# Four moves in a two-layer FoX/YOCO trunk: GpSimd's computing in written order, half a panel behind a panel's reads, a hidden block's steps, and two products of a query pair

## The chip, the cores and the metric

One core of one Trainium2 chip runs the whole program. The metric is the device time of one execution in microseconds (us); the time of a kernel is the median of its runs.

## The reference

The input x is (1, 256, 2048) in float32; there are 16 heads of 128 and two layers.

```python
def sq_relu_mlp(h, g, w1, w2):
    a = jax.nn.relu(rms_norm(h, g) @ w1)
    return (a * a) @ w2
...
    for l in range(N_A):
        u = rms_norm(h, a_norm_g[l])
        proj = u @ a_w_in[l]
        q, k, v, fz = jnp.split(proj, [D, 2 * D, 3 * D], axis=-1)
        q = rms_norm(q.reshape(B, S, H, Dh), a_q_g[l])
        k = rms_norm(k.reshape(B, S, H, Dh), a_k_g[l])
        v = v.reshape(B, S, H, Dh)
        logf = jax.nn.log_sigmoid(fz.astype(jnp.float32) + a_b_f[l].astype(jnp.float32))
        o = forgetting_attention(q, k, v, logf)
        h = h + o.reshape(B, S, D) @ a_w_out[l]
        h = h + sq_relu_mlp(h, mlp_norm_g[layer], mlp_w1[layer], mlp_w2[layer])
        layer += 1
    kv = rms_norm(h, kv_norm_g) @ kv_w
    k_sh, v_sh = jnp.split(kv, [D], axis=-1)
    k_sh = rms_norm(k_sh.reshape(B, S, H, Dh), kv_k_g)
    v_sh = v_sh.reshape(B, S, H, Dh)
    for l in range(N_B):
        u = rms_norm(h, b_norm_g[l])
        q = rms_norm((u @ b_w_q[l]).reshape(B, S, H, Dh), b_q_g[l])
        o = chunked_relbias_attention(q, k_sh, v_sh, b_rel[l])
        h = h + o.reshape(B, S, D) @ b_w_out[l]
        h = h + sq_relu_mlp(h, mlp_norm_g[layer], mlp_w1[layer], mlp_w2[layer])
        layer += 1
    return h
```

The first layer attends causally with a bias made of summed log forget gates; the second attends in chunks of 64 with a learned bias by distance. N_A and N_B are 1, D is 2048, the hidden width of the MLP is 8192.

## The kernel before, in words

**Products.** All weights and activations are float32 and are split into a high and a low part: ACT writes the high part of a tile (`hi`, L323), DVE subtracts it from the tile and writes the low part (`lo`, L324). A product then takes three passes over TensorE, each a run of matmuls of 512 columns: high activation by high weight (L592), low activation by high weight (L594), high activation by low weight (L596). A run has four matmuls in an ordinary product and two in a product of a pair (below). The unit of weight is 128x1024, 512 KB; a unit's three passes of four matmuls each use one `hi` and one `lo`. Three `hi` and three `lo` buffers go round.

**Pairs.** Part of the weight columns are taken in pairs (`Pair`) by a scheme of the Strassen-Winograd kind. Four panels, 12, 22, 21 and 11, give seven products: 12, 11, 21, 22 and those of the sums T3 (22 and 12), T1 (12 and 11), T2 (T3 and 11) and T4X`bring` (L937) issues a panel's load on SP; `make` (L965) forms a sum on DVE; `put` (L975) forms one with an accumulating DMA that GpSimd issues, which reads the second panel from memory and adds it to the tile; T4 of an MLP's pair is made this way, each half when DVE has split T2's half. In an MLP the panels are twice as wide (128x2048, 1 MB) and are used in halves of 1024 columns. When "V" is in `p.has`, DVE (L1017) has formed the accumulator that the pair's later products add to; the code asserts this before ordinary products of the second column ("b early").

**Order of the work.** `plan` lists pairs and ordinary units in the order in which TensorE takes them; `run` walks that list and issues everything in program order. Ahead of a pair, `prepare(p, d)` counts down the ordinary units still to come (d) and brings or makes each panel at the count that a row of a table of numbers sets for it (`units`, in the order 12, 22, 21, 11, T3, T1; here `p.units[1]` is that of panel 22). `FO` sets the order of the last three products of a pair by kind of pair: "4" is panel 21's product, "5" is T4's and "6" is 22's; where a kind has no entry the order is 456. Kinds are named by `p.order`: "second" is the pair at each MLP's opening, "query" the pair of the second layer's query projection.

**Fill.** Everything that isn't a product (norms, attention, hidden blocks) is cut into small steps in the list `fill`; `run_fill` issues one entry after each product. So a step's entry says between which products its instructions stand on their engine.

- A head norm (`head_norm`, L660 to L674) squares on ACT, sums on DVE (L663), scales and adds on DVE (L667), raises to the power -1/2 on GpSimd (L668, tile `ss`), and scales rows on ACT (L674, `qn`). It does so for two blocks of rows.
- The bias of a head group in the first layer (`decay_bias`) is loaded by a DMA on GpSimd (L911, tile `nb`) and masked by two GpSimd instructions (L913, L916); DVE reads it at L738. In the second layer (`rel_bias`) tile `rb` is loaded (L1229), a corner is set by a GpSimd MEMSET (L1231), and DVE copies part of it (L1233).
- A turn (`carry`) writes a tile to memory (L450) and reads it back in four pieces in another order (L456), both on SP's queue. The activations of an MLP's input come so: y<-q (L417), act<-y (L420) on ACT, then act<-y on DVE (L421). A hop (`hop`, L466) does the same for a hidden block by 16 small copies within the core, on SP's and GpSimd's queues.
- A hidden block of an MLP (`take`): after its hop ACT applies relu (L1038), squares into the high part (L1043) and squares in place (L1045); DVE subtracts (L1049), and four sums (L395 to L398) with their split (L402, L405) prepare what the pairs' products with sums need. A row of a table gives the entries of hop, reads, relu, square, square, subtract and sums: `T0H` for the first block of the first MLP, `T0K` for that of the second.

**What pins the order.** At the end `keep_order(tc, engines)` (L88) adds a dependency from each instruction to the next one on its engine, for DVE, ACT, TensorE and SP, so that the scheduler keeps these four in written order. GpSimd isn't among them: there the scheduler may set a ready instruction ahead of one that was written earlier.

Of the kernel before, what the change touches and what calls it, by code (L numbers as in the profile page):

```python
# [27 lines left out]
UN = 1024  # L28
# [1 line left out]
TABLES = {  # L30
    "ATA": ((10, 13, 15, 19, 9), (9, 12, 15, 18, 12), (8, 13, 15, 19, 9), (9, 9, 12, 12, 9)),
    "ATB": ((11, 12, 14, 18, 9), (9, 13, 15, 17, 11), (9, 12, 15, 17, 10), (7, 10, 12, 12, 10)),
# [27 lines left out]
    "SHORT": ((4, 0, 0, 4, 7, 7, 7, 8, 11), (2, 2, 3, 3, 7, 7, 8, 11, 13), (4, 0, 0, 2, 6, 6), (0, 0, 1, 2, 4, 5)),  # L60
# [24 lines left out]
WIDE2 = (0, 1, 2, 3, 4, 5, 6, 7)  # L85


def keep_order(tc, engines):  # L88

    last = {}  # L90
    for i in tc.nc.cur_bb.bb.instructions:
        if i.engine in engines:
            if i.engine in last:
                tc.add_manual_dep(i, last[i.engine], mybir.DependencyInfo(mybir.DependencyClass.NoSync, mybir.DependencyReason.DATA),
                                  reason="written order")
            last[i.engine] = i.name
# [3 lines left out]
def trunk(ctx: ExitStack, tc: tile.TileContext, xT, xr, gs, hg, bf, wgate, w_in, w_oa, w1a, w1fa, w1sa, w2fa, w2sa,  # L100
          w_kv, w_qb, w_ob, w1b, w1fb, w1sb, w2fb, w2sb, rel, out):
    nc = tc.nc
    V, S, G, TE, SY = nc.vector, nc.scalar, nc.gpsimd, nc.tensor, nc.sync
# [305 lines left out]
    def room(tag, name, dtype=F32):  # L409
        return qkv.tile([P, DEEP], dtype, name=name, tag=tag, bufs=1)  # L410
# [63 lines left out]
    query = []  # L474
# [445 lines left out]
    def bring(p, name):  # L920
        if p.order == "out1":
            i = int(name in ("11", "21"))
            if i not in p.box:
                p.box[i] = acts.tile([P, DEEP], F32, name="wB", tag="act")
            p.t[name] = p.box[i][:, name[0] == "2" and UN or 0 :][:, :UN]
        elif p.order in LAZY:
            f, n = owner.get(p.rooms[name], (None, None))
            assert f is None or {"12": "T1", "21": "21", "11": "11", "22": "22"}[n] in f.issued, ("room busy", name, n)
            assert n != "11" or "T2" in f.has
            owner[p.rooms[name]] = p, name  # L930
            p.t[name] = sub(p.rooms[name])[:, UN:]
        elif p.order == "":
            p.t[name] = sub(p.rooms[name])[:, :UN]
        else:
            p.t[name] = room(p.rooms[name], "w" + name)
        p.has.add(name)
        SY.dma_start(p.t[name][:, : p.cols], p.big[name])  # L937

    def make(p, name, half=None):
        t = p.t  # L940
        if half == 1:
            pass
        elif name == "T3":
            if p.order in ("query", ""):
                t[name] = query_room(0)
            elif p.order == "kv0":
                t[name] = query_room(3)
            elif p.order in LAZY:
                t[name] = acts.tile([P, 2 * UN], F32, name="wT3", tag="act")[:, :UN]
            else:  # L950
                t[name] = prob.tile([P, 4 * UN], F32, name="wT3", tag="p", bufs=1) if p.order == "early" else room("bias", "wT3")
        else:
            t[name] = t[{"T1": "12", "T2": "T3", "T4": "11"}[name]]
        a, b = {"T1": ("12", "11"), "T3": ("22", "12"), "T2": ("T3", "11"), "T4": ("21", "T2")}[name]
        cols = slice(0, p.cols) if half is None else slice(half * UN, min(half * UN + UN, p.cols))
        d, a, b = (t[i][:, cols] for i in (name, a, b))
        if name == "T3":
            assert {"22", "12"} <= p.has and "T1" not in p.has, "T3 order"
        if name == "T1":
            assert "T30" in p.has and "T31" in p.has, ("T1 order", p.order, p.has, p.units, getattr(p, "at", 0))  # L960
        for k in (0, 1):
            if half in (None, k):
                p.has.add(name + str(k))
        p.has.add(name)
        V.tensor_tensor(d, a, b, op=ALU.add)  # L965
# [9 lines left out]
        G.dma_start(p.t[name][:, cols], p.big[other][:, cols], accum_op=ALU.add)  # L975

    def prepare(p, d):
        if p.deep and d == p.units[4] - 1:
            make(p, "T3", 1)
        for name, at in zip(("12", "22", "21", "11", "T3", "T1"), p.units):  # L980
            if d == at and p.deep and name == "T3":
                make(p, "T3", 0)
            elif d == at:
                (bring if name[0] != "T" else put if p.adds and name == "T1" else make)(p, name)

    def run(plan, open_pair, masks=None, follow=None):
        starts = [i for i, it in enumerate(plan) if it[1:] == (2, 0)] + ([len(plan)] if follow else [])
        for i, (p, q, u) in enumerate(plan):
# [24 lines left out]
            else:  # L1013
# [10 lines left out]
                for nxt in [j for j in starts if j > i][: 2 if follow else 1]:  # L1024
                    d = sum(1 for it in plan[i:nxt] if it[1] < 2)
                    prepare(plan[nxt][0] if nxt < len(plan) else follow, d)
# [69 lines left out]
    def sub(tag):  # L1096
        if tag not in halves_of:
            halves_of[tag] = room(tag, "R")
        return halves_of[tag]
# [33 lines left out]
    def heads(out):  # L1133
# [34 lines left out]
        def after():  # L1168
            prepare(plan_h[0][0], box[0])
            box[0] -= 1  # L1170
# [107 lines left out]
        return f  # L1278

    mlp(plan_b, x3, S3, st3, store)  # L1280
    keep_order(tc, (V.engine, S.engine, TE.engine, SY.engine))


def _cols_a(w, swap=False):
# [79 lines left out]
```

## Time and profile before

| | |
|---|---|
| Median of 3 runs | 2054.43 us (2053.61 to 2055.51) |
| The profiled execution's own time | 2056.59 us |
| Its span, first to last instruction | 2054.8 us |
| TensorE's granted clock | 1.000 |
| Busy: TensorE, DVE, ACT, GpSimd | 99%, 87%, 68%, 12% of the span |
| Moved by DMA | 557.78 MB, mean 271 GB/s |

An execution's time includes some 1.8 us around the span. In the rows of the timeline the columns are the start and the duration in us, the engine, the line of the kernel, the operation, the tile written and the tiles read, and the shape; x4 at the end counts neighbouring instructions of one form that are shown as one. In brackets stand the idle time of the engine before the row and what ended it, as far as the profile can tell. SPq is SP's DMA queue; PEld is the loading of weights into TensorE.

### The profile page before, as it was taken

The page shows a single profiled execution, that of the slowest core. Times are in us where ns is not written, and L with a number is a line of the kernel's source. Part 1 is how long each engine was busy: PE and PEld are TensorE (multiplying, and loading weights), DVE is VectorE, ACT ScalarE, POOL GpSimd, SP SyncE. Part 2 cuts the span into 40 slices and gives each one's busy share as a digit, 9 for nine tenths or more (in the row PEclk, how much of TensorE's full clock was granted, in tenths as well). Part 3 has the DMA queues.
Part 4 walks back from the last instruction along what each step waited for, and adds up shares of the span by engine and source line. Part 5 has one row for each costly group of instructions (what it writes and reads, how often), then busy time and mean ns, then how long its engine had stood idle before and what let it go on. Part 6 is the DMA issues. An engine that isn't in the chain of part 4 may idle for free.

```text
span 2054.8 us, 27097 instructions
## 1 busy us (share of the span) xinstructions
PE 2043.5 (99%) x9062; PEld 1689.0 (82%) x9062; DVE 1786.1 (87%) x2065; ACT 1404.5 (68%) x1805; POOL 248.3 (12%) x351
## 2 busy tenths in 40 slices
PE   9999999999999999999999999999999999999999
PEld 8888878878888888888878888888888888888887
DVE  7788888899898899899988787889988988988996
ACT  7766666677677676677778666667866676776764
POOL 1121010021111102101012111100111111111020
PEclk9999999999999999999999999999999999999999
DMA  8898898898888898898889989888998888888984
GB/s 321 261 296 275 264 275 248 295 272 262 300 258 281 259 300 275 242 294 272 264 245 300 275 251 282 260 267 282 289 292 266 270 262 292 261 285 262 296 260 148
DMA packets 175021, 557.78 MB, mean 271 GB/s; under 512 B 40592, under 2 KB 69152, under 8 KB 152096
## 3 DMA queue, kind: packets, MB, share of 16 engines
q1 hardware_dynamic: 153824, 464.99, 64.3%
q0 software_dynamic: 20768, 90.75, 22.7%
q8 instruction: 71, 1.16, 0.2%
q14 instruction: 70, 0.57, 0.1%
q10 hardware_dynamic: 288, 0.30, 0.0%
HBM read 516.07 MB, written 27.29 MB: 264 GB/s over the span
## 4 chain that ended last, share of the span: by engine, by line
PE 92%; DMA 3%; DVE 2%; issue 2%; ACT 1%; POOL 0%; SPq 0%; DVEq 0%; ACTq 0%; POOLq 0%
PE acc L596 21%; PE acc L592 21%; PE acc L594 21%; PE s L596 9%; PE s L592 9%; PE s L594 9%; DVE lo L324 1%; PE po L729 1%; PE po L766 1%; DMA w<-in_w1fb 0%; DMA q<-turn 0%; ACT hi L323 0%; DMA w<-in_w2fa 0%; DMA query<-in_w_qb 0%; PE po L728 0%
## 5 line engine op out<-in xcount | busy, mean ns | idle before, releaser
L324 DVE TENSOR_TENSOR lo<-raw,hi 128x1024 fp32r<-128x1024 f32 (+1 forms) x409 | 494.8, 1214 | 81.3 <-ACT hi L323 77.4
L323 ACT ACTIVATE hi<-raw 128x1024 fp32r<-128x1024 f32 (+1 forms) x409 | 429.6, 1054 | 188.7 <-PE acc L594 130.9
L592 PE MATMUL acc<-hi,act 128*128 128x512 f32 x1774 | 496.4, 393 | 2.1 <-ACT hi L323 1.0
L596 PE MATMUL acc<-lo,act 128*128 128x512 f32 x1774 | 491.1, 390 | 1.7 <-DVE lo L324 1.5
L594 PE MATMUL acc<-hi,act 128*128 128x512 f32 x1774 | 490.4, 389 | 0.1
L596 PEld LDWEIGHTS acc<-lo,act 128*128 128x128 f32 x1774 | 332.2, 188 | 73.6 <-DVE lo L324 4.6
L594 PEld LDWEIGHTS acc<-hi,act 128*128 128x128 f32 x1774 | 332.9, 188 | 70.1 <-DVE act L421 0.5
L592 PEld LDWEIGHTS acc<-hi,act 128*128 128x128 f32 x1774 | 331.5, 188 | 71.2 <-ACT hi L323 2.5
L323 ACT ACTIVATE hi<-w 128x1024 fp32r<-128x1024 f32 x254 | 267.0, 1058 | 123.2 <-PE acc L594 81.4
L324 DVE TENSOR_TENSOR lo<-wT,hi 128x1024 fp32r<-128x1024 f32 x220 | 267.1, 1222 | 66.5 <-ACT hi L323 61.7
L324 DVE TENSOR_TENSOR lo<-w,hi 128x1024 fp32r<-128x1024 f32 x254 | 305.8, 1219 | 14.7 <-ACT hi L323 12.5
L323 ACT ACTIVATE hi<-wT 128x1024 fp32r<-128x1024 f32 x220 | 232.2, 1060 | 101.9 <-PE acc L594 43.5
L592 PE MATMUL s<-hi,act 128*128 128x512 f32 x530 | 146.5, 392 | 2.2 <-ACT hi L323 2.2
L596 PE MATMUL s<-lo,act 128*128 128x512 f32 x530 | 145.1, 389 | 0.1
L594 PE MATMUL s<-hi,act 128*128 128x512 f32 x530 | 144.8, 388 | 0.0
L466 POOL DMA_DIRECT2D q<-z x192 | 95.5, 510 | 252.5 <-DVE z L440 216.4
L592 PEld LDWEIGHTS s<-hi,act 128*128 128x128 f32 x530 | 98.9, 188 | 23.2 <-ACT hi L323 3.1
L596 PEld LDWEIGHTS s<-lo,act 128*128 128x128 f32 x530 | 99.1, 188 | 21.3 <-DVE lo L324 1.0
L594 PEld LDWEIGHTS s<-hi,act 128*128 128x128 f32 x530 | 99.4, 188 | 20.6
L592 PE MATMUL s<-hi,S 128*128 128x512 f32 x288 | 89.6, 392 | 0.0
L594 PE MATMUL s<-hi,S 128*128 128x512 f32 x288 | 88.7, 389 | 0.0
L596 PE MATMUL s<-lo,S 128*128 128x512 f32 x288 | 88.7, 389 | 0.0
(217 smaller groups left out, 2291.4 us busy)
## 6 DMA issues: line engine op xcount, KB each, us to landing
raw<-in_w_in SPq DMA_DIRECT2D x75, 512.0 KB, 5.9
w<-in_w2fa SPq DMA_DIRECT2D x32, 1024.0 KB, 6.2
w<-in_w2fb SPq DMA_DIRECT2D x32, 1024.0 KB, 6.5
w<-in_w1fa SPq DMA_DIRECT2D x28, 1024.0 KB, 7.0
w<-in_w1fb SPq DMA_DIRECT2D x28, 1024.0 KB, 7.4
raw<-in_w2sa SPq DMA_DIRECT2D x52, 512.0 KB, 7.1
raw<-in_w2sb SPq DMA_DIRECT2D x50, 512.0 KB, 7.4
raw<-in_w_kv SPq DMA_DIRECT2D x48, 512.0 KB, 5.3
```

Of the source, the lines that this page charges most:

```text
L323: S.activation(hi[:, c], raw[:, c], AF.Copy)
L324: V.tensor_tensor(lo[:, c], raw[:, c], hi[:, c].bitcast(F32), op=ALU.subtract)
L466: (G if i % 2 else SY).dma_start(dst[32 * j : 32 * j + 32, i * n : (i + 1) * n], z[32 * i : 32 * i + 32, j * n : (j + 1) * n])
L592: TE.matmul(ps[:, cols], xh, cut(hi, j), start=first, stop=False, **kw)
L594: TE.matmul(ps[:, cols], xl, cut(hi, j), start=False, stop=False, **kw)
L596: TE.matmul(ps[:, cols], xh, cut(lo, j), start=False, stop=last, **kw)
L729: TE.matmul(s[:, P : 3 * P], q[:, a, P:T], k[:, a], start=True, stop=True)
L766: TE.matmul(po[:, :T], v[:, 0, a * P : (a + 1) * P], pT[:, :2], start=True, stop=False)
```

## The change

The change does four things.

1. `keep_order` also takes GpSimd, all but its DMAs: its computing instructions stay in written order among themselves.
2. In a pair of kind "second" (one in each MLP) the load of panel 11 is cut in two. The first 1024 columns are issued where the whole panel was, the second 1024 when panel 22 comes up, just ahead of it. In the first MLP the four reads of a turn lie between these places.
3. In the first row of `T0H`, relu goes from entry 6 to 5 and the sums' first step from entry 6 to 7; the entries of hop, squares, subtraction and the split of the sums stay.
4. `FO` gets an entry for "query": T4's product goes behind 22's, "465" in the place of the default.

```diff
-    "FO": {"second": "456", "ahead1": "456", "ahead0": "456", "deep1": "456", "deep0": "465"},
+    "FO": {"second": "456", "ahead1": "456", "ahead0": "456", "deep1": "456", "deep0": "465", "query": "465"},
...
-    "T0H": ((1, -1, 6, 6, 6, 6, 6, 8, 8), (0, -1, 4, 5, 6, 6, 7, 8, 8), (0, 4, 6, 7, 7, 7), (1, -1, 5, 5, 5, 5)),
+    "T0H": ((1, -1, 5, 6, 6, 6, 7, 8, 8), (0, -1, 4, 5, 6, 6, 7, 8, 8), (0, 4, 6, 7, 7, 7), (1, -1, 5, 5, 5, 5)),
...
-def keep_order(tc, engines):
+def keep_order(tc, engines, compute):
 
     last = {}
     for i in tc.nc.cur_bb.bb.instructions:
-        if i.engine in engines:
+        if i.engine in engines or i.engine == compute and "DMA" not in type(i).__name__:
...
         p.has.add(name)
-        SY.dma_start(p.t[name][:, : p.cols], p.big[name])
+        if p.order == "second" and name == "11":
+            p.has.add("11 half")
+            SY.dma_start(p.t[name][:, :UN], p.big[name][:, :UN])
+        else:
+            SY.dma_start(p.t[name][:, : p.cols], p.big[name])
...
     def prepare(p, d):
+        if d == p.units[1] and "11 half" in p.has:
+            p.has.remove("11 half")
+            SY.dma_start(p.t["11"][:, UN : p.cols], p.big["11"][:, UN : p.cols])
...
-    keep_order(tc, (V.engine, S.engine, TE.engine, SY.engine))
+    keep_order(tc, (V.engine, S.engine, TE.engine, SY.engine), G.engine)
```

The lines behind L934 move by 4, those behind the start of `prepare` by 7: `put` is L979 after the change, relu L1045.

On GpSimd, at the last head group of the first layer, before the change (cd is the bias in memory, `wT` and `R` are tiles of pairs):

```order
L975 DMA R<-in_w_oa 128x1024
L911 DMA nb<-cd 128x1536
L668 TENSOR_TENSOR ss<-ss,mhalf 128x4
L913 AFFINE_SELECT nb<-nb 128x4x128
L916 AFFINE_SELECT nb<-nb 128x4x128
L668 TENSOR_TENSOR ss<-ss,mhalf 128x4
L975 DMA wT_2419<-in_w_oa 128x1024
```

And after it, at the same place:

```order
L979 DMA R<-in_w_oa 128x1024
L911 DMA nb<-cd 128x1536
L668 TENSOR_TENSOR ss<-ss,mhalf 128x4 x2
L913 AFFINE_SELECT nb<-nb 128x4x128
L916 AFFINE_SELECT nb<-nb 128x4x128
L979 DMA wT_2419<-in_w_oa 128x1024
```

The second power goes ahead of the two masks. In head groups 1 and 2 the masks go behind both powers of the next norm likewise, and in the first group of the second layer the MEMSET of `rb` goes behind two more pairs of powers.

On SP, at the opening of the first MLP (w_3683 is panel 11, w_3717 panel 22), before:

```order
L450 DMA turn<-z 128x1024
L937 DMA w_3683<-in_w1fa 128x2048
L299 DMA raw<-in_w1a 128x1024
L456 DMA q<-turn 32x4x256 x4
L937 DMA w_3717<-in_w1fa 128x2048
L299 DMA raw<-in_w1a 128x1024
```

And after (panel 22 is w_3718 here):

```order
L450 DMA turn<-z 128x1024
L939 DMA w_3683<-in_w1fa 128x1024
L299 DMA raw<-in_w1a 128x1024
L456 DMA q<-turn 32x4x256 x4
L984 DMA w_3683<-in_w1fa 128x1024
L941 DMA w_3718<-in_w1fa 128x2048
L299 DMA raw<-in_w1a 128x1024
```

Half of panel 11 goes behind the four reads and a raw block. In the second MLP the second half goes behind the reads and two raw blocks in the same way.

On DVE, at the first hidden block of the first MLP (L1017 forms an accumulator; `w` and `wT` are a pair's panel and T4), before:

```order
L1049 TENSOR_TENSOR act<-q,act 128x1024
L395 TENSOR_TENSOR sum<-q 128x256
L396 TENSOR_TENSOR sum<-q,sum 128x256
L397 TENSOR_TENSOR sum<-q 128x256
L398 TENSOR_TENSOR sum<-q,sum 128x256
L324 TENSOR_TENSOR lo<-w_3754,hi 128x1024
L1017 TENSOR_TENSOR s<-s,p_3941 128x512
L324 TENSOR_TENSOR lo<-wT_3800,hi 128x1024 x2
```

And after:

```order
L1056 TENSOR_TENSOR act<-q,act 128x1024
L324 TENSOR_TENSOR lo<-w_3755,hi 128x1024
L1024 TENSOR_TENSOR s<-s,p_3942 128x512
L395 TENSOR_TENSOR sum<-q 128x256
L396 TENSOR_TENSOR sum<-q,sum 128x256
L397 TENSOR_TENSOR sum<-q 128x256
L398 TENSOR_TENSOR sum<-q,sum 128x256
L324 TENSOR_TENSOR lo<-wT_3801,hi 128x1024 x2
```

The four sums go behind the split of a panel's half and the accumulator. On ACT relu goes ahead of three instructions: a copy of an accumulator (L1030) and two `hi`. On TensorE, in the query pair, the two runs of T4's product and the two runs of 22's change places around one ordinary product between them.

## The prediction

> **What bounds the kernel now.** I read the page first, then the waits of TensorE, then the timeline around each of them, and the transfers of the stretch where the engines wait for one. The page's span and its row of engines:
>
> ```profile
> span 2054.8 us, 27097 instructions
> PE 2043.5 (99%) x9062; PEld 1689.0 (82%) x9062; DVE 1786.1 (87%) x2065; ACT 1404.5 (68%) x1805; POOL 248.3 (12%) x351
> ```
>
> TensorE is busy all but 11.3 us of 2054.8, and no edit removes a matmul. So the change can win only pauses of TensorE, and can lose only by making new ones. The waits of TensorE (us in total, times, the longest) name nearly all of the large ones:
>
> ```profile
> PE s L592 <- ACT hi L323: 2.2, 1, 2.2
> PE acc L596 <- DVE lo L324: 1.5, 2, 1.4
> PE acc L592 <- ACT hi L323: 1.0, 2, 0.6
> PE acc L592 <- ACT act L420: 0.9, 1, 0.9
> ```
>
> Each of the four edits sits at one of these rows. To price a pause I compare starts: when nothing waits, what follows a run of four 512-column matmuls starts 0.91 us after it (this row of the chain of waits), and what follows a run of two 0.45 us, half of it:
>
> ```profile
> 279.75 0.91 PE s L596 x4
> ```
>
> **Edit 1, GpSimd in written order.** The timeline at head group 3 (start, duration, engine, line; in brackets the idle time and its releaser):
>
> ```profile
> 268.27 1.03 POOL L668 TENSOR_TENSOR ss<-ss,mhalf 128x4 f32<-128x4 f32 x1 [2.87 <-DVE ss L667]
> 268.81 0.23 DVE L667 TENSOR_SCALAR ss<-ss,ex 128x4 f32<-128x4 f32 x1
> 271.85 0.64 POOL L913 TENSOR_SCALAR_AFFINE_SELECT nb<-nb 128x512 f32<-128x512 f32 x1 [2.55 <-DMA nb<-cd]
> 274.03 1.44 POOL L668 TENSOR_TENSOR ss<-ss,mhalf 128x4 f32<-128x4 f32 x1
> 275.51 1.14 ACT L674 ACTIVATE qn<-acc,ss 128x128 f32<-128x128 f32 x4 [3.90 <-POOL ss L668]
> 276.68 0.71 DVE L440 STREAM_TRANSPOSE z<-qn 128x512 f32<-128x512 f32 x1 [1.47 <-ACT qn L674]
> 277.62 1.23 DVE L324 TENSOR_TENSOR lo<-raw,hi 128x1024 fp32r<-128x1024 f32 x1 [0.23 <-ACT hi L323]
> 277.64 1.20 PE L592 MATMUL s<-hi,act 128*128 128x512 f32 x4 [2.21 <-ACT hi L323]
> ```
>
> The second power (ss) has its input at 269.04 (268.81 + 0.23), but stands behind two masks, and the first of these waits until 271.85 for its DMA. ACT is free at 271.61 (275.51 less 3.90) and idle until qn; the split hi<-raw is queued behind qn, and TensorE waits for it: 2.21 us, and a slow start, 1.20 us for the 0.91 of a run of four. That makes 2.5 us. Changed, the second power runs from 269.30 to 270.3 or 270.7 (1.03 or 1.44 long), before ACT is free. qn starts at 271.61 and all behind it on ACT 3.9 us sooner: hi<-raw ends near 273.7, and TensorE is due at 275.43 (277.64 less 2.21). Late next is DVE's half of that split: it ends at 278.85 now, and without the 1.47 us of idle time for qn and the 0.23 us for hi at 277.15; the third pass is due at 277.25 (275.43 and two passes of 0.91). It just fits. I take 2.5 us, and 2.2 as the lower end.
>
> The other places where GpSimd's order changes cost nothing as long as the work that now comes later has a far reader. In the shared K/V part the MEMSET of rb goes behind two pairs of powers (the tile's row has durations, first and last start; then the timeline):
>
> ```profile
> L1233 DVE COPY rb<-rb x4: 419/420/423, 1166.2 to 1307.4; 128x512 f32<-128x512 f32 x4
> 1147.90 2.69 POOL L668 TENSOR_TENSOR ss<-ss,mhalf 128x4 f32<-128x4 f32 x2 [0.88 <-DVE ss L667]
> ```
>
> It now comes after the pair that ends at 1150.6 (1147.90 + 2.69); its reader, DVE's COPY, first runs at 1166.2: 15 us of cover. If that is gone, DVE waits at the COPY, us for us.
>
> **Edit 2, half a block behind the reads.** The MLP's opening, first a row of the windows (the stretch, its length, busy time and count of TensorE, its weight loads, DVE, ACT, GpSimd, granted clock, DMA share, GB/s), then two of its transfers (count, size, median us from issue to landing):
>
> ```profile
> 388.00:400.00 12.00, 12.00 (x55) 9.94 (x54) 7.77 (x10) 5.11 (x6) 0.00 (x0) 1.00 1.02 300
> ```
>
> ```profile
> w<-in_w1fa SPq DMA_DIRECT2D x3, 1024.0 KB, 10.3
> raw<-in_w1a SPq DMA_DIRECT2D x5, 512.0 KB, 10.8
> ```
>
> And the timeline:
>
> ```profile
> 390.44 2.12 SPq L456 DMA_DIRECT2D q<-turn  x4
> 400.83 0.91 ACT L417 ACTIVATE y<-q,gsb 128x256 f32<-128x256 f32 x2 [5.07 <-DMA q<-turn]
> 402.67 1.07 PE L596 MATMUL acc<-lo,act 128*128 128x512 f32 x4
> 404.63 1.19 PE L592 MATMUL acc<-hi,act 128*128 128x512 f32 x4 [0.90 <-ACT act L420]
> 405.87 1.23 DVE L965 TENSOR_TENSOR wT<-w,w 128x1024 f32<-128x1024 f32 x1
> 405.89 0.76 PEld L594 LDWEIGHTS acc<-hi,act 128*128 128x128 f32 x4 [0.50 <-DVE act L421]
> 407.12 1.06 ACT L323 ACTIVATE hi<-w 128x1024 fp32r<-128x1024 f32 x1 [0.65 <-PE acc L594]
> ```
>
> TensorE is due at 403.58 (402.67 + 0.91) and starts at 404.63; the next pass starts 1.26 after that instead of 0.91, with a slow start of some 0.1 again. That is 1.05 + 0.35 + 0.1 = 1.5 us, and it follows from the four reads of q, which are behind a 1 MB panel on SP's queue while the DMA engines are full (share 1.02, 300 GB/s). With 524 KB fewer ahead, at 300 GB/s the reads land 1.75 us sooner (estimate from that row; 1.3 if other queues take a quarter of the room, 2.3 at most). The passes need 1.05 and 1.4 of it, so the whole 1.5 goes. The second half pays: it lands about where the reads land now, near 400.8, and its first reader is ACT's hi<-w at 407.12. Panel 22 and the raw blocks behind it on SP's queue have as many bytes ahead as before, one more issue (0.33 us) apart; 22 is first read by DVE at 405.87. In the second MLP the same split meets no pause for reads, and is costed at nothing with the same cover.
>
> The Trainium skill speaks against the split: the page DMA: Bandwidth & Descriptors, section Rules for kernel authors, asks for 1 MiB or more in one DMA, and its section on latency puts the fixed cost of one near 2 us. Taken as time in which the queue moves nothing, that would make panel 22 some 2 us late, and the third rival below the likely one. The rows above speak against it: the stretch has five transfers of 512 KB among its three panels, and the engines are never short of work (1.02).
>
> **Edit 3, steps of the first hidden block moved.** The timeline thirty us on:
>
> ```profile
> 428.95 1.04 ACT L1038 ACTIVATE q<-q 128x1024 f32<-128x1024 f32 x1
> 432.21 1.23 DVE L1049 TENSOR_TENSOR act<-q,act 128x1024 fp32r<-128x1024 f32 x1 [1.91 <-ACT q L1045]
> 434.13 0.61 PE L594 MATMUL acc<-hi,act 128*128 128x512 f32 x2
> 434.82 1.22 DVE L324 TENSOR_TENSOR lo<-w,hi 128x1024 fp32r<-128x1024 f32 x1
> 435.95 1.06 ACT L323 ACTIVATE hi<-wT 128x1024 fp32r<-128x1024 f32 x1 [1.88 <-DMA wT<-in_w1fa]
> 436.09 0.73 PE L596 MATMUL acc<-lo,act 128*128 128x512 f32 x2 [1.35 <-DVE lo L324]
> 437.12 0.63 PE L594 MATMUL acc<-hi,act 128*128 128x512 f32 x2
> 437.83 0.72 PE L596 MATMUL acc<-lo,act 128*128 128x512 f32 x2
> 439.31 0.62 PE L596 MATMUL acc<-lo,act 128*128 128x512 f32 x2
> ```
>
> Here TensorE is due at 434.58 and starts at 436.09 (1.51); after 437.12 it is due at 437.57 and starts at 437.83 (0.26); with the two slow starts 2.0 us. With relu one slot ahead ACT's chain releases DVE 1.04 us sooner, and with the four sums (1.38 us from the end of act at 433.44 to 434.82) behind lo<-w, that lo ends some 2.4 us sooner: the first pause goes. The next ones become late: DVE is then without a gap, its sums now stand ahead of lo<-wT, and the second half of wT (T4, the accumulating DMA that GpSimd issues) is waited for by ACT at 435.95.
>
> So I price edits 2 and 3 together at this place. TensorE takes the lo of T4's second half at 439.31. If T4 lands when it does now, hi ends at 437.01 and lo 1.24 later at 438.25: 1.06 us may be won up to here in all, even though edit 2 alone had won 1.5. If T4 lands sooner by the whole 1.5 us by which its issue moves, the bound is 2.6. The DMA engines are nearly full there, so I take two thirds of it, 1.0: 2.0 us for both, of which 1.5 is edit 2's. Moving the sums costs nothing by itself: they feed the later products with sums.
>
> **Edit 4, two products of a query pair swapped.** The waits blame ACT's hi:
>
> ```profile
> 1036.00:1048.00 12.00, 11.41 (x50) 8.66 (x49) 12.00 (x14) 8.36 (x12) 0.00 (x0) 1.00 1.02 264
> 1043.03 0.61 PE L596 MATMUL acc<-lo,act 128*128 128x512 f32 x2
> 1043.40 0.69 DVE L1017 TENSOR_TENSOR acc<-acc,p 128x512 f32<-128x512 f32 x1
> 1044.23 1.17 PE L592 MATMUL acc<-hi,act 128*128 128x512 f32 x4 [0.59 <-ACT hi L323]
> ```
>
> TensorE is due at 1043.48 and starts at 1044.23: 0.75, and 0.1 in its slow start. But the waiting run is a run of four, and the products that are swapped are runs of two. The run of four is an ordinary product on the accumulator that DVE's L1017 writes until 1044.09, and DVE, busy 12.00 of 12.00 us there, has the same instructions ahead of L1017 after the swap. I take 0, between 0 and 0.85.
>
> **Sum.** 2.5 + 1.5 + 0.5 + 0 = 4.5 us. The profiled execution took 2056.59 us, so it would take 2052.1; it was 2.16 us above the median of the runs. Against the median of 2054.43 that makes 2049.9 us. 0.2%, about what a measurement of this kernel can tell from no change, is 4.1 us: the forecast is just outside it.
>
> **The rivals.**
> - *The view is right at 1043.* Then T4's product, swapped to a later place, no longer holds up TensorE, and 0.85 more goes: 2049.1 (2049.9 less 0.85). For it speaks the named releaser; against it the shape of the waiting run. Chance 0.1.
> - *T4's transfer doesn't move.* Edits 2 and 3 together win 1.06, and the sum is 3.6: 2050.9, within 0.2%. If DVE's lo at 277 is late too, 2051.2. For it speak the 1.88 us that ACT waits for wT at 435.95, and the full DMA engines. Chance 0.3.
> - *The split costs queue time.* If the second DMA leaves the queue empty for a while, all behind it is late by that. Panel 22 is issued right after the reads, at 392.6, and a panel lands 10.3 us later: by DVE's start at 405.87 it has 2.9 us to spare. T4 has nothing to spare: what it comes late eats the 2.0 us of edits 2 and 3, us for us. 0.4 us of it bring the sum within 0.2%; 2.0 or more leave edit 1: 2.5, 2051.9. For it speaks that four reads and two more issues pass SP there in a row; against it, the share of 1.02. The page's rule leads here. Chance 0.12.
> - *GpSimd's order makes others wait (slower).* A mask or MEMSET now waits for powers, which wait for DVE. In the K/V part it decides from the point where the powers end over 15 us later than 1150.6: then DVE's COPY waits, and behind it the splits that feed TensorE. One more pair of powers (2.69 us) past the cover in each of the four groups costs 10.8 and leaves 6.3 of loss: 2060.7. The cover speaks against it. Chance 0.04.
>
> **How the numbers follow.** My forecast has 0.44, the rivals 0.1, 0.3, 0.12 and 0.04. Edit 1 alone is the safest term, and alone it stays within 0.2%; to be past it, edits 2 and 3 must give 1.6 of their 2.0. So faster gets the first rival's 0.1 and nine tenths of the forecast's 0.44, 0.5 in all; same 0.46; slower 0.04. The range reaches from all bounds at their best (2.5 + 2.6 + 0.85, 2048.5) to edit 1 alone at its lower end (2.2, 2052.2).
>
> **What would show it.** Right: ss x2 ahead of the masks and no wait of ACT for it near 271; y<-q near 399; L596 of the first hidden block without a wait near 433; the wait near 1043 still there. Wrong: TensorE waiting for lo near 277, for wT's hi near 435 by over 1 us, for panel 22 near 404, or DVE idle before the COPY of rb.

## The result and the profile after

The changed kernel took 2053.12 us (median of 14 runs, 2050.59 to 2058.22); the kernel before, on the same chip, 2055.01 us (14 runs, 2052.11 to 2059.26). The ratio is 0.9984, with a 95% interval of 0.9976 to 0.9992: 3.3 us faster (1.6 to 4.9), 2051.1 us against the median of 2054.43 that the prediction starts from. That lies in the stated range and inside 0.2%, on the faster side; the forecast was 4.5 us, just past 0.2%. (In the section on the kernel, "T4X" is to be read as "T4 (T2 and 21).")

Of the changed kernel I read the same views as of the kernel before. Page and waits of TensorE (in us: total, times, longest):

```profile
span 2056.4 us, 27097 instructions
PE 2046.3 (100%) x9062; PEld 1688.9 (82%) x9062; DVE 1784.8 (87%) x2065; ACT 1403.9 (68%) x1805; POOL 247.0 (12%) x351
```

```profile
PE acc L592 <- DVE acc L1012: 2.1, 1, 2.1
PE pt L141 <- DVE mhalf L143: 1.1, 1, 1.1
PE acc L596 <- DVE lo L324: 0.8, 2, 0.6
PE acc L592 <- DVE acc L1024: 0.6, 1, 0.6
PE po L766 <- DMA pbuf<-turn: 0.4, 1, 0.4
PE acc L592 <- ACT hi L323: 0.3, 1, 0.3
```

The span is longer than that of the kernel before, though the kernel is faster: the profiled execution took 2058.22 us, the slowest of its 14. The reason is the first row, a new pause. Its place in the timeline, and the windows around it (length; busy time and count of TensorE, weight loads, DVE, ACT, GpSimd; granted clock; DMA share; GB/s):

```profile
1728.83 2.00 ACT L323 ACTIVATE hi<-w 128x1024 fp32r<-128x1024 f32 x2 [3.03 <-DMA w<-in_w2fb]
1731.90 0.70 PE L592 MATMUL acc<-hi,Sh 128*128 128x512 f32 x2 [2.05 <-DVE acc L1012]
```

```profile
1726.00:1730.00 4.00, 3.85 (x17) 2.84 (x16) 1.13 (x2) 1.17 (x2) 0.33 (x1) 1.00 1.03 383
1730.00:1734.00 4.00, 2.10 (x7) 1.73 (x8) 4.00 (x5) 3.19 (x4) 0.00 (x0) 0.88 1.07 255
1734.00:1738.00 4.00, 4.00 (x14) 3.14 (x13) 3.66 (x5) 1.22 (x2) 0.00 (x0) 0.70 0.97 331
1738.00:1742.00 4.00, 4.00 (x19) 3.31 (x18) 2.47 (x3) 2.58 (x3) 0.00 (x0) 1.00 1.00 326
```

ACT waited 3.03 us for a panel's sum in the second MLP, which GpSimd's accumulating DMA brought late, and TensorE for what follows it. After the pause it ran at a lower granted clock for 3 to 4 us. None of the four edits is near, and GpSimd's instructions are in the same order in both kernels from about 1165 us on.

Where the edits are, first head group 3 (compare 268.27 to 277.64 before):

```profile
268.09 2.92 POOL L668 TENSOR_TENSOR ss<-ss,mhalf 128x4 f32<-128x4 f32 x2 [2.88 <-DVE ss L667]
271.29 1.18 ACT L674 ACTIVATE qn<-acc,ss 128x128 f32<-128x128 f32 x4
271.86 0.64 POOL L913 TENSOR_SCALAR_AFFINE_SELECT nb<-nb 128x512 f32<-128x512 f32 x1 [0.84 <-DMA nb<-cd]
277.00 1.20 PE L596 MATMUL s<-lo,act 128*128 128x512 f32 x4
282.68 0.67 PE L766 MATMUL po<-pbuf,R 128*128 128x256 f32 x2 [0.40 <-DMA pbuf<-turn]
```

The powers are one pair ahead of the masks, and ACT no longer waits for them. In place of the pause stand two small ones: DVE's lo by 0.1 us (and a slow start of 0.1) at 277.00, and a read that had been hidden, at 282.68 (0.4 us of waiting, 0.6 with what leads up to it).

The opening of the first MLP, and its first hidden block:

```profile
388.52 2.52 SPq L456 DMA_DIRECT2D q<-turn  x4
398.21 0.91 ACT L417 ACTIVATE y<-q,gsb 128x256 f32<-128x256 f32 x2 [4.12 <-DMA q<-turn]
400.99 1.07 PE L596 MATMUL acc<-lo,act 128*128 128x512 f32 x4
402.01 1.20 PE L592 MATMUL acc<-hi,act 128*128 128x512 f32 x4
432.53 0.42 DVE L398 TENSOR_TENSOR sum<-q,sum 128x256 f32<-128x256 f32 x1
432.87 1.22 DVE L324 TENSOR_TENSOR lo<-wT,hi 128x1024 fp32r<-128x1024 f32 x1
433.57 1.06 ACT L323 ACTIVATE hi<-wT 128x1024 fp32r<-128x1024 f32 x1 [2.13 <-PE acc L594]
434.14 0.73 PE L596 MATMUL acc<-lo,act 128*128 128x512 f32 x2 [0.63 <-DVE lo L324]
```

The reads go from issue to ACT's first y in 9.69 us; before it was 10.39 (400.83 less 390.44). TensorE is due at 401.90 and starts at 402.01, and a second pause of 0.23 follows: 0.57 of the 1.50 us are left. At 434 the wait for lo<-w has gone and one of 0.63 for lo<-wT has come: DVE splits T4's first half right after the four sums. T4's transfer is not waited for: ACT's idle time before the hi of its second half ends with TensorE, which frees a buffer.

The query pair, after the swap:

```profile
1039.76 1.22 DVE L324 TENSOR_TENSOR lo<-raw,hi 128x1024 fp32r<-128x1024 f32 x1
1040.89 0.69 DVE L1024 TENSOR_TENSOR acc<-acc,p 128x512 f32<-128x512 f32 x1
1041.73 1.16 PE L592 MATMUL acc<-hi,act 128*128 128x512 f32 x4 [0.61 <-DVE acc L1024]
```

The same run of four has the same pause, and now the view names DVE's accumulator for it.

One pair of profiles therefore gives 2.4 us won up to 1480 and 3.9 lost at 1729, which is not the measured ratio. What an execution does by chance and what a kernel does had to be told apart first.

### The profile page after: what moved, and what is told of

It reads as the page before. It is cut to its first block, busy times and chain, and to the rows that moved or that the text cites. A ratio compares the mean times of both kernels' runs of the same rounds, so it can differ in the third digit from the quotient of the medians.

```text
span 2056.4 us, 27097 instructions
## 1 busy us (share of the span) xinstructions
PE 2046.3 (100%) x9062; PEld 1688.9 (82%) x9062; DVE 1784.8 (87%) x2065; ACT 1403.9 (68%) x1805; POOL 247.0 (12%) x351
## 4 chain that ended last, share of the span: by engine, by line
PE 92%; DMA 3%; DVE 3%; issue 1%; ACT 1%; SPq 0%; POOL 0%; DVEq 0%; ACTq 0%; POOLq 0%
PE acc L596 22%; PE acc L592 22%; PE acc L594 22%; PE s L596 8%; PE s L592 8%; PE s L594 8%; DVE lo L324 1%; DMA wT<-in_w1fa 1%; DMA wT<-in_w1fb 1%; PE po L729 1%; PE po L766 1%; DMA w<-in_w2fb 1%; DMA q<-turn 0%; DMA R<-turn 0%; PE po L728 0%
## 5 line engine op out<-in xcount | busy, mean ns | idle before, releaser
L592 PE MATMUL acc<-hi,act 128*128 128x512 f32 x1774 | 496.4, 393 | 0.9 <-DVE acc L1024 0.6
L592 PEld LDWEIGHTS acc<-hi,act 128*128 128x128 f32 x1774 | 331.4, 188 | 70.5 <-ACT hi L323 1.8
L592 PE MATMUL s<-hi,act 128*128 128x512 f32 x530 | 146.4, 391 | 0.0
L592 PEld LDWEIGHTS s<-hi,act 128*128 128x128 f32 x530 | 98.9, 188 | 20.5 <-ACT hi L323 0.4
L592 PE MATMUL s<-hi,S 128*128 128x512 f32 x288 | 89.5, 392 | 0.0
```

Source lines behind the costliest of these rows:

```text
L592: TE.matmul(ps[:, cols], xh, cut(hi, j), start=first, stop=False, **kw)
```

## The experiments

The theory at this point: each edit takes away its own pause, of the size in the trace. The rivals: the transfers set the pace and take back what is won; and the pauses that wait for a transfer differ from execution to execution, so that one trace doesn't give their size. Nine of the twelve runs below were timed in five rounds; the kernel before again, the changed kernel's third run and the kernel with the whole panel behind the reads are single executions.

### Each edit alone

GpSimd's order alone:

```diff
-    keep_order(tc, (V.engine, S.engine, TE.engine, SY.engine))
+    keep_order(tc, (V.engine, S.engine, TE.engine, SY.engine), G.engine)
```

> Only GpSimd's order is changed. Theory (each edit takes away its own pause and nothing else): the pause of 2.5 us near 275 shrinks to about 0.2, TensorE then waits some 0.6 us for the read pbuf<-turn near 282, so 1.6 us are won by 290, and they last: the pauses near 404 and 435 stay at 1.5 and 2.0. About 1.6 us faster than before, 0.08%. Rival (the transfers set the pace, and what is won is given back at the next read): the pause near 404 grows to about 3, and nothing is left behind it. The 1.1 us of pauses near 1150 that the changed kernel no longer had: gone here if the order of GpSimd removed them.

Ratio 0.9993 (0.9983 to 1.0003). Its waits:

```profile
PE acc L592 <- ACT act L420: 1.8, 1, 1.8
PE acc L596 <- DVE lo L324: 1.5, 2, 1.4
PE acc L592 <- DVE acc L1005: 1.2, 1, 1.2
```

The pause near 275 is gone (0.37 us are left, no read is waited for). The last row, 1.2 us, is near 1734. The pause near 404 grew to 2.4 us: this is what the rival said. But its size changes without any edit that bears on it: it is 0.80 us with the swap alone, and 1.50 and 0.86 us in two profiles of the kernel before. Nor does it grow when TensorE comes early: with 2.71 us lost near 275 (the steps alone) it is 0.81, with 0.06 lost there (the kernel before, again) 0.86. One profile doesn't exclude the rival, but the others don't bear it out. The pauses near 1150 are gone here, and also in the second profile of the kernel before and in the three other kernels with one edit, so the order isn't what removed them.

The split alone:

```diff
+        if p.order == "second" and name == "11":
+            p.has.add("11 half")
+            SY.dma_start(p.t[name][:, :UN], p.big[name][:, :UN])
...
+        if d == p.units[1] and "11 half" in p.has:
+            p.has.remove("11 half")
+            SY.dma_start(p.t["11"][:, UN : p.cols], p.big["11"][:, UN : p.cols])
```

> Only the load of panel 11 is split. Theory: the reads land about 1 us sooner against TensorE's need, as in the changed kernel, and of the 1.5 us near 404 some 0.6 are left: 0.9 us won. Rival (0.6 were left only because edit 1 had moved TensorE ahead of the transfers): the whole 1.5 goes. Either way the second MLP's opening near 1453 tells whether the split there costs something: 0.5 us before, 0.9 to 1.1 if the split is what made it longer in the changed kernel.

Ratio 0.9996 (0.9987 to 1.0005). The pause near 404 is gone, all of it, as the rival said. But the pause near 275 is gone too (0.06), though GpSimd's order is the old one here. Its rows there:

```profile
264.44 0.56 POOL L911 DMA_DIRECT2D nb<-cd  x1 [12.20 <-issue]
267.89 1.03 POOL L668 TENSOR_TENSOR ss<-ss,mhalf 128x4 f32<-128x4 f32 x1 [2.88 <-DVE ss L667]
270.37 0.64 POOL L913 TENSOR_SCALAR_AFFINE_SELECT nb<-nb 128x512 f32<-128x512 f32 x1 [1.45 <-DMA nb<-cd]
270.97 0.68 POOL L916 TENSOR_SCALAR_AFFINE_SELECT nb<-nb 128x512 f32<-128x512 f32 x1
271.62 1.01 POOL L668 TENSOR_TENSOR ss<-ss,mhalf 128x4 f32<-128x4 f32 x1
272.66 1.15 ACT L674 ACTIVATE qn<-acc,ss 128x128 f32<-128x128 f32 x4 [1.44 <-POOL ss L668]
```

The powers stand around the masks as before, ACT still waits, but 1.44 us in place of 3.90, and TensorE doesn't. The masks' DMA came sooner: from its issue to the first mask 5.9 us here (264.44 to 270.37), 7.0 in the kernel before (264.84 to 271.85). Near 1452 this kernel paused 0.63 us, 0.1 more than the kernel before; so this profile doesn't show that the split makes that place longer.

The hidden block's steps alone:

```diff
-    "T0H": ((1, -1, 6, 6, 6, 6, 6, 8, 8), ...
+    "T0H": ((1, -1, 5, 6, 6, 6, 7, 8, 8), ...
```

> Only the steps of the first hidden block are moved. Theory (DVE is the limit there: the four sums now stand ahead of the split of T4's first half): the wait of 1.5 us for lo<-w near 434 is gone and one of about 0.8 for lo<-wT stands in its place; 2.0 us of pauses become about 1.1, 0.9 won. Rival (T4's transfer is the limit): the wait is for hi<-wT and what is won is about 0.

Ratio 0.9995 (0.9986 to 1.0003). 0.91 us of pauses are left near 435 of 1.97, with DVE's lo<-wT as the one that is waited for:

```profile
436.60 0.74 PE L596 MATMUL acc<-lo,act 128*128 128x512 f32 x2 [0.63 <-DVE lo L324]
```

This is the theory's number, and the same 0.63 as in the changed kernel. Near 404 this kernel paused 0.81 us, near 275 2.7.

The swap alone:

```diff
-    "FO": {..., "deep0": "465"},
+    "FO": {..., "deep0": "465", "query": "465"},
```

> Only the query pair's two products are swapped. Theory (the run of four waits for DVE's accumulator): the pause of 0.85 us near 1043 stays, 0 won. Rival (it waits for ACT's hi of T4's product): it is gone, 0.85 won. Anything else that differs by over 0.5 us from the kernel before is not this edit's doing and shows how much an execution varies by itself.

Ratio 0.9998 (0.9989 to 1.0007). The pause near 1043 is 0.83 us: nothing won. And with no other edit the pauses near 275 and 404 are 1.84 and 0.80 us, for 2.56 and 1.50 in the first trace. The last sentence of the expectation is what decided the next runs.

The interval of each of the four single edits takes in a ratio of 1, so the times alone show none of them. What each edit does is read from the pauses in the profiles.

### The same kernels again

> The kernel before once more, for a second profile. Theory (pauses behind a transfer differ from execution to execution): the pause near 275 is anywhere between 0 and 2.7 us and the one near 404 between 0.5 and 2.4, while the 2.0 us near 435 and the 0.85 near 1043 stay within 0.1. Rival (the profile shows a fixed schedule): 2.5, 1.5, 2.0 and 0.85 again.

The kernel before, unchanged, had a span of 2051.2 us, 3.6 less than in its first profile. Its waits of TensorE:

```profile
PE acc L596 <- DVE lo L324: 1.5, 2, 1.4
PE pt L141 <- DVE mhalf L143: 1.1, 1, 1.1
PE acc L592 <- ACT hi L323: 0.7, 1, 0.7
PE acc L592 <- DVE acc L1017: 0.6, 1, 0.6
```

The wait of 2.2 us at L592 of s, the largest of the first profile, isn't there. The 1.5 for DVE's lo is. The pause near 1043 is there as well, and here the view names DVE's accumulator where it had named ACT's hi.

> The changed kernel once more, with its own profile. Theory (the pauses that wait for a transfer differ from execution to execution, those that wait for DVE don't): the wait of 0.6 us for DVE's lo near 434 and the 0.83 us near 1041 are there again within 0.1 us; the pause of 2.2 us near 1729 with its lower clock, the 0.6 us near 282 and the 1 us near 1452 are there at random, and the 1729 one most likely not. Rival (the change itself made the pause near 1729 by putting TensorE ahead of the transfers): it is there again, 2 us or more.

The changed kernel again: ratio 0.9985 (0.9976 to 0.9993), the first result once more. Span 2050.6 us. No pause near 1729, near 404 or near 282; 0.90 near 434 and 0.85 near 1041.

> The changed kernel, for a third profile. Theory (what waits for DVE is fixed, what waits for a transfer is chance): 0.9 us of pauses near 434 with the wait for lo<-wT, 0.85 near 1041; nothing near 404 or up to 0.6; near 275 and 282 up to 1.1; no pause near 1729. Rival (the lead makes the pause near 1729): it is there.

Span 2054.8. Again nothing near 404, 282 and 1729, 0.91 near 434, 0.84 near 1041. But 4.3 us near 1452, the second MLP's opening, of which 2.1 are a wait for hi<-wT and the rest a lower clock behind it (0.80 and 0.78 in two windows of 4 us).

### What the changed kernel still waits for

The four sums one entry later, behind the split of T4, and their own split with them:

```diff
-    "T0H": ((1, -1, 5, 6, 6, 6, 7, 8, 8), ...
+    "T0H": ((1, -1, 5, 6, 6, 6, 8, 9, 9), ...
```

> The changed kernel with the four sums of the first hidden block one more entry later, behind the split of T4's two halves, and their own split later too. Theory (DVE's order is the limit that edit 3 left): the wait of 0.63 us for lo<-wT near 434 goes, and of the 0.9 to 1.6 us of pauses between 425 and 445 at most 0.3 are left. Rival (T4's transfer is the limit): TensorE waits there as long, but for hi<-wT.

Ratio 0.9992 (0.9983 to 1.0001), no better than the changed kernel. Around 432:

```profile
431.42 1.06 ACT L323 ACTIVATE hi<-wT 128x1024 fp32r<-128x1024 f32 x1 [2.49 <-DMA wT<-in_w1fa]
432.51 1.23 DVE L324 TENSOR_TENSOR lo<-wT,hi 128x1024 fp32r<-128x1024 f32 x1 [1.37 <-PE acc L596]
432.53 0.74 PE L592 MATMUL acc<-hi,act 128*128 128x512 f32 x2
```

The wait of 0.63 is gone. In its place TensorE waits for T4's second half after all (0.65 us with lo and slow starts) and then for DVE, which has the sums to do later: pauses near 436, 447 and 451, so 0.95 us between 425 and 445 and 1.54 more up to 470, where the changed kernel had 0.3 to 0.45. Both sides were right about a part. DVE's order was the next limit, and behind it come T4's landing and DVE's own work; in this one profile moving the sums only moves where it is paid.

DVE's accumulator of the query pair formed before the split that stood ahead of it:

```diff
+            early_v = p.fast and p.order == "query" and (q, u) == (0, p.own)
+            if early_v:
+                V.tensor_tensor(p.ps[1][1], p.ps[1][0], p.t["P7"], op=ALU.add)
+                p.has.add("V")
             hi, lo = ready.popleft()[:2] if q > 1 and ready and not p.deep else fetch()
...
-                if p.fast and (q, u) == (0, p.own):
+                if p.fast and (q, u) == (0, p.own) and not early_v:
```

> The changed kernel with DVE's accumulator of the query pair formed one split earlier, ahead of lo<-raw (1.1 us). Theory (the run of four near 1041 waits for that accumulator): the pause of 0.85 us is gone. Rival (it waits for ACT's hi or a transfer, as the waits of the kernel before said): the pause stays at 0.8.

Ratio 0.9987 (0.9978 to 0.9996). The place:

```profile
1038.90 0.62 PE L592 MATMUL acc<-hi,act 128*128 128x512 f32 x2
1039.04 0.69 DVE L998 TENSOR_TENSOR acc<-acc,p 128x512 f32<-128x512 f32 x1
1039.64 1.21 DVE L324 TENSOR_TENSOR lo<-raw,hi 128x1024 fp32r<-128x1024 f32 x1
1040.26 1.07 PE L592 MATMUL acc<-hi,act 128*128 128x512 f32 x4
```

The run of four starts 1.36 us (three runs of two) after 1038.90, without a pause: the 0.85 us are gone, and the releaser is settled. The whole time can't show 0.85 us, since the interval is 1.8 us either way.

All of panel 11 behind the reads:

```diff
-            SY.dma_start(p.t[name][:, :UN], p.big[name][:, :UN])
...
-            SY.dma_start(p.t["11"][:, UN : p.cols], p.big["11"][:, UN : p.cols])
+            SY.dma_start(p.t["11"][:, : p.cols], p.big["11"][:, : p.cols])
```

> The changed kernel with all of panel 11 behind the reads. Theory (half is enough; what goes behind is hidden): no pause near 404, as with half, and the hi of panel 11, first needed at about 404, not late. Rival (the bytes behind the reads come due): a new wait for hi<-w or wT of 0.5 us or more between 403 and 412.

One execution, 2050.40 us. No pause near 404 and none up to 412: panel 11 and panel 22 were in time.

```profile
387.54 1.75 SPq L456 DMA_DIRECT2D q<-turn  x4
393.35 0.91 ACT L417 ACTIVATE y<-q,gsb 128x256 f32<-128x256 f32 x2
```

The reads reach ACT in 5.81 us, and ACT doesn't wait for them.

The split in the first MLP alone, and that with the accumulator first:

```diff
-        if p.order == "second" and name == "11":
+        if p.order == "second" and name == "11" and p.units == TABLES["W1IH"]:
```

> The changed kernel with panel 11 split in the first MLP alone. Theory (the split in the second MLP costs now and then at T4's transfer): 0.5 us of pauses between 1445 and 1460, as in all kernels without the split, and on average 0.3 to 0.5 us less than the changed kernel. Rival (chance): no difference that can be told.

> The changed kernel with DVE's accumulator of the query pair one split earlier (as before) and panel 11 split in the first MLP alone. Theory: 0.85 us less than the changed kernel near 1041 and none of the 1.1 to 2.5 us near 1452 that two profiles of kernels with the split had: 0.9977 to 0.9982 of the kernel before. Rival (the pauses near 1452 are a transfer's chance and have nothing to do with the split): only the 0.85 us, 0.9980 to 0.9985, and 1452 may have a pause again.

Ratios 0.9986 (0.9977 to 0.9994) and 0.9983 (0.9974 to 0.9992). Neither has a pause near 1452 beyond the usual 0.5. The second has no pause near 1041 and 1.2 us near 1725. It beats the kernel before, and can't be told from the changed kernel. Its ratio is in the span that the rival gave, but the measured interval covers both sides, so neither expectation is decided by time.

### All profiles side by side

How late TensorE's starts are at six places, against its spacing where nothing waits, in us (sums over starts that are late by over 0.05; the first column has the place of the nb masks and the read after them, the last two the opening of the second MLP and the place near 1729):

```
                         275-282   404   435  1043  1452  1729
before                      2.56  1.50  1.97  0.83  0.52  0.00
before, again               0.06  0.86  1.96  0.82  0.52  0.00
GpSimd's order alone        0.37  2.42  1.98  0.82  0.53  1.47
split alone                 0.06  0.00  1.98  0.84  0.63  0.00
steps alone                 2.71  0.81  0.91  0.84  0.52  0.71
swap alone                  1.84  0.80  1.96  0.83  0.52  0.00
changed                     1.06  0.57  1.60  0.85  1.09  3.89
changed, again              0.06  0.00  0.90  0.85  0.52  0.00
changed, third              0.06  0.00  0.91  0.84  4.28  0.00
sums later                  0.06  0.00  0.95  0.85  2.46  0.41
accumulator first           0.42  0.00  0.90  0.00  0.53  0.00
split in first MLP only     0.06  0.00  0.90  0.82  0.53  0.00
both of these               0.06  0.00  0.90  0.00  0.53  1.17
whole panel behind          0.06  0.00  0.91  0.82  0.53  0.00
```

The span less all late starts of an execution is the same in the fourteen profiles to 0.8 us, so late starts of TensorE are what their spans differ by.

Two columns have hardly any spread within a kernel: 435 and 1043, where TensorE waits for DVE (the one exception is the 1.60 of the changed kernel's first profile, where three more starts were late by 0.7 us together). The others, where something waits for a transfer, spread within one kernel: by 2.5 us at the first place, and by 3.8 and 3.9 us at the last two, the lower clock included. By the mean of the columns edit 1 is worth 1.2 us (1.45 in the five profiles with the old order, 0.25 in the nine with the new), edit 2 also 1.2 (1.28 in the five without the split, 0.07 in the eight with half of it), edit 3 1.0 (1.97 to 0.99, the one with the sums later left out), edit 4 nothing: 3.4 us in all, for 3.3 and 3.1 measured. The means of edits 1 and 2 rest on five draws of a spread and are uncertain by some 0.6 and 0.3 us (the standard errors of those five), and the sum leaves out the last two columns, so that it agrees so closely is in part luck. The four ratios of the single edits add up to 0.18%, 3.7 us, with an error about as large.

## Why the prediction was right or wrong

- **Edit 1, the mechanism: right.** The powers pass the masks, ACT's wait is gone, and with the new order the masks' transfer no longer holds up ACT. One duration was too small: beside DVE's lo<-raw the second power takes 1.9 us in all nine profiles with the new order, for the 1.03 or 1.44 of the working. The pair ends at 271.01, still ahead of qn at 271.29, so nothing came of it. **Its size: wrong, 2.5 for 1.2.** The step that failed is "That makes 2.5 us": it took the pause of one execution for the kernel's. That execution was 2.16 us above the median, as the prediction itself noted, and this pause was part of the reason. How late the nb transfer lands decides how long it is. From its issue to the first mask the five profiles with the old order have 4.8 and 5.9 us (no pause), 6.7 (1.84), 7.0 (2.56) and 7.2 (2.71).
- **"It just fits" at 277:** DVE's lo came 0.1 us late in the profile of the changed kernel, with a slow start 0.2 us; GpSimd's order alone shows the same. In these two profiles the masks come late enough that lo<-R (1.47 and 1.48 us) and S (1.72 in both) are held up on DVE, against 1.18 and 1.28 in the split alone; the working had no term for that. In addition the changed kernel's execution waited for a read that wasn't foreseen (0.4 at 282.68). In six of the nine profiles with the new order neither is there, and their sum is 0.06.
- **Cover of the MEMSET and the masks: right.** No kernel with the new order has a pause at the readers of the masks or of the MEMSET. In the changed kernel the MEMSET runs at 1146.31 and its reader at 1162.52. The slower rival was priced for four groups, but the MEMSET changes its place in the first group alone.
- **Edit 2: right, and by about its price.** The estimate was that half a panel brings the reads 1.75 us sooner. From issue to ACT's first y they take 10.3 us on average with the whole panel ahead (five profiles, 9.3 to 11.6), 8.2 with half (eight, 7.0 to 9.7) and 5.8 with none (one): 2.1 us sooner with half, inside the bound of 2.3, which was stated without its working. The pause was again larger in the first trace (1.50) than on average (1.28). What the Trainium skill, page DMA: Bandwidth & Descriptors, section Rules for kernel authors, says against the split (1 MiB or more in one DMA) didn't show in the first MLP: in the eight profiles with half, TensorE doesn't wait for panel 11 or 22 there.
- **Edit 3: its term too small, 0.5 for 1.0.** The step that failed is the limit by T4's transfer ("I take two thirds of it, 1.0: 2.0 us for both, of which 1.5 is edit 2's"). T4 landed early enough. What stood at 434 was the other thing the prediction had named and not priced, the sums ahead of lo<-wT: 0.63 us of waiting for DVE, whether or not edit 2 is there. So edit 3 gives 1.0 us and edit 2 keeps its own: 2.2 for both, for 2.0 forecast, by another sum. T4 becomes a limit only in the kernel that moves the sums one entry further.
- **Edit 4: right, shown.** The pause stays at 0.82 to 0.85 in all twelve profiles that keep DVE's order, and is 0.00 in the two with the accumulator first. The shape of the waiting run was the better witness than the releaser in the view; in a second profile the view named DVE by itself.
- **The rivals.** "T4's transfer doesn't move" gives a sum of 3.6, near the measured one, but its mechanism didn't happen. "The split costs queue time" didn't happen in the first MLP. In the second it is open: three of the seven profiles of kernels with a split (or the whole panel behind) there show 1.1 to 4.3 us near 1452, waiting for T4's transfer, and none of the seven without. By luck alone that would come about one time in ten; the times of the kernel split in the first MLP alone and of the changed kernel can't be told apart. The prediction costs the split there "at nothing"; if the difference is real, it costs 0.9 us on average (1.43 in the seven, 0.52 in the others), and 2.5 us are left of the 3.4. "GpSimd's order makes others wait" didn't occur.
- **Sum.** 2.5 + 1.5 + 0.5 + 0 was forecast, 1.2 + 1.2 + 1.0 + 0 found. The first term was 1.3 us too high and the second 0.3; that the third was 0.5 too low made up for part of it. So two of the four terms were off by a factor of two, in opposite directions, and that the total still lies in the range is in part luck. The prediction gave 0.5 to a gain past 0.2% and 0.46 to one within; it came out within, and the oversized first term is why.

The pause near 1729 that made the profiled execution slow isn't in every execution of the changed kernel: it is absent in its two other profiles, and kernels with one edit, GpSimd's order or the steps alone, have 1.5 and 0.7 us there. No edit touches that place. Whether the change makes the pause more frequent by putting TensorE ahead of the transfers isn't shown either way.

## What to carry to other kernels

A pause that ends with a transfer is one draw of a spread, and the profiled execution's largest pause is likely a bad draw: take a second profile of the same kernel before its length becomes a term of the sum. A pause that ends with a computing engine that is busy without a gap came out here the same to 0.1 us in all but one profile, so it could be priced from one. And when an edit removes a wait, price first what the busy engine does next in its own order; the transfer behind it comes after that.

## What the runs showed of the hardware

- **GpSimd's masks and DVE's two-input instructions hold each other up.** In the first profile of the kernel before:

```profile
264.84 0.56 POOL L911 DMA_DIRECT2D nb<-cd  x1 [12.23 <-issue]
272.29 1.28 DVE L324 TENSOR_TENSOR lo<-R,hi 128x1024 fp32r<-128x1024 f32 x1
272.45 1.61 POOL L916 TENSOR_SCALAR_AFFINE_SELECT nb<-nb 128x512 f32<-128x512 f32 x1
273.49 1.71 DVE L405 TENSOR_TENSOR S<-sum,S 128x512 fp32r<-128x512 f32 x2
```

  With the split alone the same two on DVE:

```profile
272.29 1.18 DVE L324 TENSOR_TENSOR lo<-R,hi 128x1024 fp32r<-128x1024 f32 x1
273.39 1.28 DVE L405 TENSOR_TENSOR S<-sum,S 128x512 fp32r<-128x512 f32 x2
```

  The late mask begins under lo<-R and takes 1.61 us for 0.68, and the power beside S takes 1.44 for 1.01, S itself 1.71 for 1.28. So the transfer's 1.1 us more (7.0 for 5.9 from issue to the first mask) became 2.0 us more at the second power (9.2 for 7.2). The Trainium skill, page SBUF — State Buffer, section Who interferes with whom, has this as a lock: a DVE instruction with two inputs in SBUF and a GpSimd instruction that reads SBUF share a port, and the later one waits. The rows agree, and so do the other profiles: in the six in which the second mask starts after lo<-R it takes 1.61 or 1.62 us, in the eight in which it starts before 0.63 to 0.68. In two of these eight (the swap alone, and the split in the first MLP only) lo<-R starts under the mask and takes 1.58 and 1.59 us itself.
- **A pause of 2.05 us can cost the clock, one of 2.21 need not.** The pause at 1731.90 was followed by windows at 0.88 and 0.70, and some 1.7 us of slow matmuls on top of it; the one at 277.64 before was followed by windows at 1.00. The Trainium skill, page TensorE: Matmul & The Clock Gate, section What's actually happening, puts the window of the clock gate near 3.4 us, has it run freely, and gives one idle window as what slows the clock. Here a pause shorter than one window was enough.

  The traces' own record of the granted clock tells the two pauses apart. Its stretches are whole multiples of 3.41 us long (in the changed kernel's first profile 1727.14, 3.41 and 320.85 us), and in the fourteen profiles it fell only twice between start-up and end, to half for 3.41 us each: 1.1 us after this pause ended, and 0.5 us after the pause of 1.89 us near 1453 in the changed kernel's third profile. Laid on this grid of 3.41 us, TensorE was idle for 2.05 and 1.95 us of the interval just before. The pauses of 2.21 us and, with the steps alone, 2.37 us are cut by the grid into 1.36 and 0.85, and 1.64 and 0.72 us. So in these profiles the idle time within one interval decides, and not the length of the pause; where between 1.64 and 1.95 us the limit lies, no run shows.
